# First mixer of a two-block transformer kernel: HGRN2's values third among the column groups, its states and outputs in the key's pieces

## The chip, the cores and the metric

The kernel runs on one core of a Trainium2 chip. The metric is the device time of one execution in microseconds (us), taken as the median of repeated runs. A core has TensorE (PE in the profile; its weight loads are PEld), VectorE (DVE), ScalarE (ACT), GpSimd (POOL), SyncE (SP), which here only issues transfers, and 16 DMA engines.

## The reference

Two blocks of two layers each work on a sequence of 256 tokens of width 1024, all in 32-bit floats. The change touches only the first layer of the first block, the "even mixer":

```
h = x @ w_in                                  # 1024 -> 3584 = seven groups of 512 columns
qa, ka, va, hq, hf, hi, hg = split(h)         # groups 0 .. 6
o_a = diff_attention(qa, ka, va, ...)         # 4 heads: two softmaxes, their difference times v, rms norm
o_b = hgrn2(hq, hf, hi, hg, ...)              # 4 heads, chunks of 64 tokens
mix = concat(o_a, o_b) @ w_out
```

HGRN2 is a gated linear recurrence. From `hq` and `hf` (query and forget gate) it forms decayed queries and keys per chunk of 64 tokens; with the values `hi` it forms the chunk's own output and a state that is carried from chunk to chunk; the result is rms-normed and multiplied by silu(`hg`). After the mixer come a layer norm, a feed-forward part and a gate, then the second layer, then the second block, which also has a second sequence (the "context") of 256 tokens.

## The kernel before, in words

**Tiling.** The 256 tokens are two tiles of 128 (index `t`). Every large product is computed as three fp32r matmuls (high by high, high by low, low by high), since each operand is split into a high and a low part. Weights come as units of 512 KB: `WeightStream.emit` (L208) issues the load on SP's queue, ACT casts the high part (L214), DVE subtracts to get the low part (L216). Units are consumed in program order, at most four ahead. One column group of `w_in` is a "chunk" (`chunk`, L700): four units, each 12 matmuls of 128x512 (L279 to L281), into two PSUM banks of the tag `acc`, one for each `t`. After the fourth unit the chunk's evacuation function runs for both `t`.

**Order.** The program is a list of items; an item is a unit with its matmuls, or a function without weights (`do`). `weave(a, b)` (L236) spreads the items of `b` evenly over those of `a`; with `ahead=True` the items of `b` come before the item of `a` that they are spread to. The list gives priorities only: the framework (`schedule_with_timeline_sim=True`) fixes each engine's order of instructions when the program is built, from its own estimate of times, so an item whose inputs it expects late can be passed by a later one. On the chip each engine then keeps that order.

**The even mixer** (L505) has these items beside its seven chunks:
- `hg1a`, `hg1b`, `hg1c` (L560 to L600), once for each `t`: the cumulated decays, decayed queries and keys, and masked scores. They need `hf` and `hq`. They leave three tiles of the tag `t2` for each `t` (decayed query, decayed key, masked scores).
- `hg2` (L607), once for each `t`: output of the chunk's own tokens (L613), state increments (L619), the state recurrence on DVE (L623, L626), the output from earlier states (L633), all into one `acc` bank, which ACT copies out (L636). It needs `hg1c` and the values `vv` that `evac_hi` (L602) copies out of chunk 5.
- `da`: nine items that run eight steps of differential attention, four heads with t=0 and then four with t=1, as a pipeline of two stages. `da1` (L671): scores for two softmaxes into the two `sc` banks (L676), masks and maxima on DVE (L485), exponentials on ACT (L488), the weighted difference on DVE (L678 to L680). `da2` (L683): PE transposes into the one `sm` bank and a DVE copy (L689). Item i runs `da1` of step i and `da2` of step i-1.
- `da_out(t)` (L691): the product with the values into an `acc` bank (L696), then `out_norm` (L639): squares on ACT (L420), a power on GpSimd (L385), two products on DVE (L643, L644), transposes, split into the operand of the output projection.
- `evac_hg` (L650), at the end of chunk 6: silu on ACT (L652), then `out_norm` of what `hg2` left.

**Buffers.** PSUM has eight banks: four `acc`, two `sc`, one `sm`, one `fil`. The tag `t2` has ten buffers (attention's scores, rope, norms and the tiles from `hg1` all take them), `a4` six.

**Around it.** `block1_layer` weaves fifteen further items over the mixer's list of 49: parts of the second block's modulation (`modulation`, L938: a 512 KB load each of `w_mod` into one of two `fr` buffers, matmuls L957 into `fil`) and the norm and transposes of the two context tiles (`ctx_first`'s `norm`, L1385, which also take `fr` and `fil`). The tenth and eleventh of the fifteen are the context norms, the last four are modulation. Behind the mixer's list stands the first chunk of the context's own projection (four units, 48 matmuls with input `mh`), and then the mixer's output projection `ev_w_out`.

The order that the program gives before the change: chunk 4 (`hf`), 3 (`hq`), then 0 and 1 (query, key) with `hg1` spread over them, then 2 and 5 (value, `hi`) with `da[0..5]` and `da_out(0)`, then 6 (`hg`) with `da[6..8]`, `hg2(0)`, `hg2(1)` and `da_out(1)`.

Of the kernel before, what the change touches and what calls it, by code (L numbers as in the profile page):

```python
# [119 lines left out]
def body(ctx: ExitStack, tc: tile.TileContext, A: dict, out: bass.AP):  # L120
# [112 lines left out]
    def do(fn, *args):  # L233
        return ((), lambda: fn(*args))

    def weave(a, b, ahead=False):  # L236

        out, j = [], 0
        for i, it in enumerate(a):
            if not ahead:  # L240
                out.append(it)
            while j < len(b) and (j + 1) * len(a) <= (i + 1) * len(b):
                out.append(b[j])
                j += 1
            if ahead:
                out.append(it)
        return out + b[j:]
# [20 lines left out]
    def proj(w, kdim, chunks, xs, evac, t_outer=(), tag="acc", first=0):  # L268
        new = tag if callable(tag) else lambda: PT(tag)

        items = []

        nu = kdim // 2

        def mms(o, x, wt, u):
            (xh, xl), (wh, wl) = x, wt
            for kk in range(2):
                k = 2 * ((u + first) % nu) + kk
                mm(o, xh[:, k, :], wh[:, kk, :], start=(u == 0 and kk == 0), stop=False)  # L279
                mm(o, xh[:, k, :], wl[:, kk, :], start=False, stop=False)  # L280
                mm(o, xl[:, k, :], wh[:, kk, :], start=False, stop=(u == nu - 1 and kk == 1))  # L281

        for ci, (c0, n) in enumerate(chunks):
            units = [(w, 2 * ((u + first) % nu), 2, c0, n) for u in range(nu)]
            if ci in t_outer:
                def whole(*wts, ci=ci, n=n):
                    for i, x in enumerate(xs()):
                        ps = new()[:, 0:n]
                        for u in range(nu):
                            mms(ps, x, wts[u], u)  # L290
                        evac(ci, i, ps)

                items.append((units, whole))
            else:
                held = []
                for u in range(nu):
                    def part(wt, ci=ci, n=n, u=u, held=held):
                        x = xs()
                        if u == 0:
                            held.extend(new()[:, 0:n] for _ in x)  # L300
                        for i in range(len(x)):
                            mms(held[i], x[i], wt, u)
                        if u == nu - 1:
                            for i in range(len(x)):
                                evac(ci, i, held[i])

                    items.append(([units[u]], part))
        return items
# [184 lines left out]
    def pipeline(steps, *stages):  # L493

        got = {}

        def at(i):
            for n, f in enumerate(stages):
                if 0 <= i - n < len(steps):
                    got[i - n] = f(*steps[i - n], *got.pop(i - n, ()))  # L500

        return [do(at, i) for i in range(len(steps) + len(stages) - 1)]


    def even_mixer(xs, y, ynew):  # L505
# [194 lines left out]
        def chunk(i, ev, t_outer=()):  # L700
            return proj(w, 8, [(512 * i, 512)], xs, ev, t_outer)

        da = pipeline([(h, t) for t in range(2) for h in range(4)], da1, da2)
        def consts():
# [5 lines left out]
        hf.insert(2, do(consts))  # L710
        return (
            [do(setup)] + hf + chunk(3, evac_hq)
            + weave(chunk(0, evac_q) + chunk(1, evac_k), [do(f, t) for t in range(2) for f in (hg1a, hg1b, hg1c)])
            + weave(chunk(2, evac_v) + chunk(5, evac_hi), da[:6] + [do(da_out, 0)])
            + weave(chunk(6, evac_hg), da[6:] + [do(hg2, 0), do(hg2, 1), do(da_out, 1)], ahead=True)
        ), []


# [1010 lines left out]
```

## Time and profile before

| what | value |
|---|---|
| median of 3 runs | 1923.53 us (1917.25, 1923.53, 1923.91) |
| the profiled execution: its time, its span | 1920.0 us, 1918.2 us |
| mean granted TensorE clock | 0.981 of full speed |
| PE busy | 1842.1 us, 96% of the span, 12481 matmuls |
| DVE busy | 1224.2 us, 64% |
| ACT busy | 988.7 us, 52% |
| POOL busy | 51.0 us, 3% |
| DMA | 338.84 MB, mean 177 GB/s |

The span runs from the first to the last instruction; 1.8 us of the execution lie around it. A busy share is the time in which an engine has an instruction in flight. The mixer takes roughly the first 175 us of the span.

### The profile page before, as it was taken

Reading aid. Unit: us, or ns where it says so; the run is one execution under the profiler, and the core shown is the slowest. Engines: PE = TensorE matmul, PEld = TensorE weight load, DVE = VectorE, ACT = ScalarE, POOL = GpSimd, SP = SyncE. Lnnn points to the kernel's source line nnn. Section 1 sums busy time; section 2 is a strip of 40 time slices with the busy share of each in tenths; the row PEclk is TensorE's granted clock in tenths of the full one; section 3 lists DMA queues with packets and bytes.
Section 4 is the critical chain, followed back from the end, with each engine's and each line's share of the span. In section 5 each row is a group of like instructions: output and inputs, shape, how many; then the busy total and the mean of one; then the engine's idle time right before and its main releaser. Section 6 shows DMA issues by size and latency. Waiting matters only on the chain. (4 is left out here: it accounts for less than half of the span.)

```text
span 1918.2 us, 31907 instructions
## 1 busy us (share of the span) xinstructions
PE 1842.1 (96%) x12481; PEld 1574.4 (82%) x12481; DVE 1224.2 (64%) x2333; ACT 988.7 (52%) x1630; POOL 51.0 (3%) x74
## 2 busy tenths in 40 slices
PE   7999999999999899999899999999999999989997
PEld 5766888997887688888787889899898886669997
DVE  5565656656666666668577876685646666755545
ACT  5463564554565364544568553454546556344443
POOL 1000000000000000000000000000000000000000
PEclk9999999999999899999899999999999999989999
DMA  8746654545756554465353355556665464456652
GB/s 282 253 162 212 217 184 144 176 154 192 220 167 198 191 189 151 169 219 174 118 170 103 122 163 167 168 182 192 195 212 168 153 187 146 140 177 187 184 181 98
DMA packets 100835, 338.84 MB, mean 177 GB/s; under 512 B 11572, under 2 KB 12812, under 8 KB 100684
## 3 DMA queue, kind: packets, MB, share of 16 engines
q1 hardware_dynamic: 100140, 336.43, 54.3%
q8 instruction: 98, 1.61, 0.3%
q0 software_dynamic: 544, 0.36, 0.2%
q14 instruction: 53, 0.43, 0.1%
HBM read 335.70 MB, written 1.05 MB: 176 GB/s over the span
## 5 line engine op out<-in xcount | busy, mean ns | idle before, releaser
L216 DVE TENSOR_TENSOR wl<-wr,wh 128x1024 fp32r<-128x1024 f32 (+3 forms) x562 | 638.0, 1137 | 412.6 <-ACT wh L214 406.0
L214 ACT CAST wh<-wr 128x1024 fp32r<-128x1024 f32 (+3 forms) x562 | 549.6, 981 | 655.5 <-PE acc L281 134.6
L279 PE MATMUL acc<-wh,mh 128*128 128x256 f32 (+3 forms) x400 | 132.0, 336 | 3.5 <-ACT mh L378 2.0
L280 PE MATMUL acc<-wl,mh 128*128 128x256 f32 (+3 forms) x400 | 130.8, 329 | 0.7 <-DVE wl L216 0.7
L281 PE MATMUL acc<-wh,ml 128*128 128x256 f32 (+3 forms) x400 | 131.1, 330 | 0.0
L279 PE MATMUL acc<-wh,xh 128*128 128x512 f32 (+3 forms) x304 | 117.0, 394 | 6.1 <-ACT xh L378 3.8
L280 PE MATMUL acc<-wl,xh 128*128 128x512 f32 (+3 forms) x304 | 117.9, 388 | 2.5 <-DVE wl L216 2.5
L281 PE MATMUL acc<-wh,xl 128*128 128x512 f32 (+3 forms) x304 | 117.4, 387 | 0.1
L850 PE MATMUL acc<-wh,a 128*128 128x512 f32 x256 | 102.4, 403 | 0.0
L851 PE MATMUL acc<-wl,a 128*128 128x512 f32 x256 | 101.9, 398 | 0.0
L852 PE MATMUL acc<-wh,a 128*128 128x512 f32 x256 | 101.6, 398 | 0.0
L1473 PE MATMUL sc<-xh,wh 128*128 128x256 f32 x352 | 99.7, 284 | 0.0
L1474 PE MATMUL sc<-xl,wh 128*128 128x256 f32 x352 | 99.5, 283 | 0.0
L1475 PE MATMUL sc<-xh,wl 128*128 128x256 f32 x352 | 99.5, 283 | 0.0
L1474 PE MATMUL sc<-ml,wh 128*128 128x256 f32 x352 | 99.1, 282 | 0.0
L1473 PE MATMUL sc<-mh,wh 128*128 128x256 f32 x352 | 98.9, 281 | 0.0
L1475 PE MATMUL sc<-mh,wl 128*128 128x256 f32 x352 | 98.4, 279 | 0.0
L279 PEld LDWEIGHTS acc<-wh,mh 128*128 128x128 f32 x400 | 75.2, 189 | 14.1 <-issue 3.2
L280 PEld LDWEIGHTS acc<-wl,mh 128*128 128x128 f32 x400 | 75.7, 189 | 6.6 <-DVE wl L216 1.3
L281 PEld LDWEIGHTS acc<-wh,ml 128*128 128x128 f32 x400 | 75.6, 189 | 6.7 <-issue 0.6
L279 PEld LDWEIGHTS acc<-wh,xh 128*128 128x128 f32 x304 | 58.1, 193 | 22.8 <-ACT wh L214 4.6
L825 PE MATMUL sc<-mh,wh 128*128 128x256 f32 x256 | 74.6, 293 | 1.6 <-DVE ml L358 1.6
(570 smaller groups left out, 4683.4 us busy)
## 6 DMA issues: line engine op xcount, KB each, us to landing
wr<-in_ffn_w_dram SPq DMA_DIRECT2D x128, 512.0 KB
fr<-in_w_mod_dram SPq DMA_DIRECT2D x90, 512.0 KB
wr<-in_w_gate_dram SPq DMA_DIRECT2D x66, 512.0 KB
wr<-in_w_up_dram SPq DMA_DIRECT2D x66, 512.0 KB
wr<-in_w_down_dram SPq DMA_DIRECT2D x66, 512.0 KB
wr<-in_w_in_dram SPq DMA_DIRECT2D x40, 384.0 KB
wr<-in_ev_w_in_dram SPq DMA_DIRECT2D x28, 512.0 KB
wr<-in_w_in_dram SPq DMA_DIRECT2D x28, 512.0 KB
```

The lines of the kernel that those rows point to most:

```text
L214: S.copy(hi, raw)
L216: V.tensor_tensor(lo, raw, hi, ALU.subtract)
L279: mm(o, xh[:, k, :], wh[:, kk, :], start=(u == 0 and kk == 0), stop=False)
L280: mm(o, xh[:, k, :], wl[:, kk, :], start=False, stop=False)
L281: mm(o, xl[:, k, :], wh[:, kk, :], start=False, stop=(u == nu - 1 and kk == 1))
L825: mm(o, wh[:, kk, bs], mh, start=(k == 0 and b % 2 == 0), stop=False, skip_group_check=True)
L850: mm(o, hh[:, b, ts_], wh[:, kk, :], start=(b == 0), stop=False)
L851: mm(o, hh[:, b, ts_], wl[:, kk, :], start=False, stop=False)
L852: mm(o, hl[:, b, ts_], wh[:, kk, :], start=False, stop=(b == 3))
L1473: mm(o, wh[:, kk, bs], mh, start=(k == 0 and b == 0), stop=False, skip_group_check=True)
L1474: mm(o, wh[:, kk, bs], ml, start=False, stop=False, skip_group_check=True)
L1475: mm(o, wl[:, kk, bs], mh, start=False, stop=(k == 7), skip_group_check=True)
```

## The change

Chunk 5 (`hi`) moves from fifth to third place, so that it and chunk 0 (query) carry the `hg1` items; `hg2(0)` and `hg2(1)` move from chunk 6 into chunk 1 (key); chunk 2 (value) carries the first three attention items instead of chunk 2 and 5 carrying six and `da_out(0)`; chunk 6 carries the other six, `da_out(0)` and `da_out(1)`. No instruction is added or removed by the source, and no tile or buffer count is changed.

```diff
@@ -710,9 +710,10 @@
         hf.insert(2, do(consts))
         return (
             [do(setup)] + hf + chunk(3, evac_hq)
-            + weave(chunk(0, evac_q) + chunk(1, evac_k), [do(f, t) for t in range(2) for f in (hg1a, hg1b, hg1c)])
-            + weave(chunk(2, evac_v) + chunk(5, evac_hi), da[:6] + [do(da_out, 0)])
-            + weave(chunk(6, evac_hg), da[6:] + [do(hg2, 0), do(hg2, 1), do(da_out, 1)], ahead=True)
+            + weave(chunk(5, evac_hi) + chunk(0, evac_q), [do(f, t) for t in range(2) for f in (hg1a, hg1b, hg1c)])
+            + weave(chunk(1, evac_k), [do(hg2, 0), do(hg2, 1)])
+            + weave(chunk(2, evac_v), da[:3])
+            + weave(chunk(6, evac_hg), da[3:6] + [do(da_out, 0)] + da[6:] + [do(da_out, 1)], ahead=True)
         ), []
```

Written out, with u0 to u3 for a chunk's units, the end of the mixer's list was

```
chunk 2: u0, u1, da0, u2, da1, u3, da2        chunk 5: u0, da3, u1, da4, u2, da5, u3, da_out(0)
chunk 6: da6, u0, da7, da8, u1, hg2(0), u2, hg2(1), da_out(1), u3
```

and becomes

```
chunk 1: u0, u1, hg2(0), u2, u3, hg2(1)       chunk 2: u0, u1, da0, u2, da1, u3, da2
chunk 6: da3, da4, u0, da5, da_out(0), u1, da6, da7, u2, da8, da_out(1), u3
```

The mixer's list has 49 items in both, so the fifteen items of `block1_layer` keep their places in the count: the context norms come behind items 32 and 35 (before: `da3` and chunk 5's u2; now: `da0` and chunk 2's u3), the last four modulation parts behind items 39, 42, 45 and 48.

## Rows read from the trace of the kernel before

**Rows 1.** Busy time by 10 us windows: PE, PEld, DVE, ACT, POOL, PEclk, DMA share, GB/s.
```profile
110.00:120.00 10.00, 10.00 (x47) 7.12 (x47) 4.51 (x15) 4.28 (x12) 0.57 (x1) 1.00 0.35 120
120.00:130.00 10.00, 6.69 (x31) 4.55 (x30) 7.33 (x25) 7.83 (x20) 0.56 (x1) 0.79 0.17 52
130.00:140.00 10.00, 10.00 (x60) 7.42 (x59) 8.45 (x23) 7.17 (x21) 1.02 (x1) 0.87 0.51 143
140.00:150.00 10.00, 9.86 (x76) 6.65 (x75) 7.50 (x24) 3.41 (x9) 0.00 (x0) 1.00 0.89 320
150.00:160.00 10.00, 7.50 (x64) 4.76 (x63) 2.48 (x8) 2.70 (x10) 0.81 (x1) 1.00 0.68 215
```

**Rows 2.** Waits of PE from 120 to 160 us: total, times, longest.
```profile
PE fil L177 <- ACT t L488: 2.1, 1, 2.1
PE fil L957 <- DMA fr<-in_w_mod_dram: 1.3, 2, 0.7
PE fil L177 <- DVE t L377: 1.0, 1, 1.0
PE acc L279 <- ACT t L636: 0.7, 1, 0.7
PE sm L619 <- DVE a L689: 0.5, 1, 0.5
```

**Rows 3.** Timeline of PE, 119 to 133 us: start, length, what (idle before).
```profile
119.33 0.60 PE L177 MATMUL fil<-ident,fr 128*128 128x128 f32 x4
...
122.50 0.70 PE L676 MATMUL sc<-a,a 64*128 64x256 f32 x2
123.37 0.70 PE L676 MATMUL sc<-a,a 64*128 64x256 f32 x2 [0.18 <-DVE mx L485]
126.14 1.09 PE L177 MATMUL fil<-ident,fr 128*128 128x128 f32 x4 [2.07 <-ACT t L488]
...
128.97 1.09 PE L177 MATMUL fil<-ident,fr 128*128 128x128 f32 x4 [1.02 <-DVE t L377]
129.71 0.78 PE L279 MATMUL acc<-wh,xh 128*128 128x512 f32 x1
...
132.42 0.46 PE L279 MATMUL acc<-wh,xh 128*128 128x512 f32 x1
132.72 0.40 PE L280 MATMUL acc<-wl,xh 128*128 128x512 f32 x1
132.95 0.40 PE L281 MATMUL acc<-wh,xl 128*128 128x512 f32 x1
```

**Rows 4.** Timeline of PE, end of chunk 6 to the context's projection.
```profile
141.27 0.39 PE L281 MATMUL acc<-wh,xl 128*128 128x512 f32 x1
...
156.81 0.43 PE L633 MATMUL acc<-t,t 128*64 128x128 f32 x2
157.92 0.50 PE L279 MATMUL acc<-wh,mh 128*128 128x512 f32 x1 [0.68 <-ACT t L636]
```

**Rows 5.** Timeline of ACT near 157 us.
```profile
157.28 0.59 ACT L636 COPY t<-acc 128x512 f32<-128x512 f32 x1 [9.68 <-PE acc L633]
...
158.93 1.28 ACT L652 ACT_TABLE_LOAD   x1
```

**Rows 6.** Timeline of DVE: the end of one attention step.
```profile
126.73 0.48 DVE L680 SCALAR_TENSOR_TENSOR t<-t,rs 128x256 f32<-128x256 f32 x1
...
128.75 0.41 DVE L689 COPY a<-sm 128x256 f32<-128x256 f32 x1
```

**Rows 7.** PE's modulation matmuls from 122 to 158 us, by line and form.
```profile
L957 PE MATMUL fil<-fr,cT 128*32 128x256 f32 x64 | 4.9, 390 | 1.4 <-DMA fr<-in_w_mod_dram 1.3
```

**Rows 8.** Timeline of ACT around an earlier table load.
```profile
49.55 1.04 ACT L214 CAST wh<-wr 128x1024 fp32r<-128x1024 f32 x1
50.61 1.28 ACT L567 ACT_TABLE_LOAD   x1
51.90 0.60 ACT L567 ACTIVATE t<-sm 128x512 f32<-128x512 f32 x1
```

## The prediction

> **What bounds the kernel now.** I read the windows of the first 230 us first, because the change can only act there. PE is the bound: in all eight 10 us windows from 40 to 120 us it is busy for all 10.00 us at a granted clock of 1.00 (the last of the eight stands in [rows 1]). So whatever is moved between 40 and 120 us changes nothing there: PE does the same matmuls in another order. Then come two pockets. In the window at 120 us PE is busy for 6.69 us and the clock is 0.79, in the next the clock is 0.87; at 150 us it is busy for 7.50 us.
>
> The second view is PE's waits from 120 to 160 us [rows 2]: 2.1 and 1.0 us for context transposes, 1.3 us for modulation loads, 0.7 us for ACT's copy of HGRN2's output, 0.5 us for attention's DVE copy. By the windows the idle time is 3.3 + 0.1 + 2.5 = 5.9 us [rows 1].
>
> The third is PE's timeline. **First pocket:** scores of an attention step go out at 122.50 and 123.37, then PE's queue has context transposes in front, whose input is late, and no matmul of chunk 6 ahead of them; chunk 6 starts at 129.71 [rows 3]. After that gap the clock is at the lower of its two levels (1.2 of 2.4 GHz): the first six matmuls of chunk 6 take 132.42 - 129.71 = 2.71 us, where six at the later pitch of 0.23 take 1.38, and two groups of four transposes last 1.09 us where an earlier one lasted 0.60 [rows 3]. That is 1.3 + 1.0 = 2.3 us, beside 3.3 us of idle time. **Second pocket:** chunk 6's last matmul is at 141.27; from there PE has only small matmuls until 157.92, when the context's own projection starts, right after ACT's copy of the second HGRN2 output [rows 4, 5]. In the code this is a matter of `acc` banks: chunk 6 holds two until `evac_hg` has run, which needs what `hg2` left; `hg2(0)`, `hg2(1)` and `da_out(1)` want the others; so the context's 48 matmuls, ready as far as their weights go, have no bank. Idle time here is 2.5 us.
>
> **The change, part by part.** No instruction comes or goes, so the ceiling of a gain within the mixer is what the pockets lose: 5.9 + 2.3 = 8.2 us, 0.43% of 1923.5.
>
> 1. *`evac_hi` and `hg2` go forward.* Their matmuls (L613, L619, L633) leave the second pocket and enter chunk 1, where PE is full. The dense work there moves back by as much; on PE this costs nothing and gains nothing by itself. What is gained is that at the end chunk 6's two banks are freed as soon as its silu has run, that `da_out` has a bank, and that the context's projection can go on PE while attention ends. Six of the ten `t2` buffers, which `hg1` leaves occupied until `hg2`, are free before attention starts. Of the 2.5 us of the second pocket the 0.7 us for ACT's copy and the 0.5 us for L689 [rows 2] should go; the 1.3 us for loads stay, since the last four modulation parts and the loads on SP's queue keep their place in the count. Taken: -1.2 us, between 0 and -2.5.
>
> 2. *Attention goes backward.* Five of its eight score steps and both `da_out` now stand in chunk 6; before, two score steps and one `da_out`. The serial length of a step is read from the one that starts at 122.50: its difference ends at 126.73 + 0.48 = 127.21, its copy at 128.75 + 0.41 = 129.16 [rows 3, 6], so 4.7 us to the difference and 6.7 us to the copy. Its cover is chunk 6, 141.27 - 129.71 = 11.6 us long [rows 3, 4], the modulation's 4.9 us [rows 7], four groups of context transposes of 0.6 us, 2.4 us [rows 3], and then the context's projection. If steps overlap as the two stages allow, five of them fit under 11.6 + 4.9 + 2.4 = 18.9 us, that is 3.8 us a step, and the rest under the context's 48 matmuls at 0.23 us, 11.0 us. I take 0, between 0 and the price in the rival below.
>
> 3. *Context norms keep their count.* Behind the second of them there now are four dense units (chunk 6), before five (chunk 5's u3 and chunk 6). So the first pocket can come back in another place: its cause, transposes in an in-order queue ahead of work that could run, is not removed. But chunk 6 finds `acc` banks more easily, since HGRN2's are not asked for any more, and ACT no longer has `evac_hi` between context and chunk 6. I take half of 3.3 + 2.3 = 5.6 us: -2.8, between 0 and -5.6.
>
> 4. *Loads.* All 28 units of this weight are equally big and come in equal number; SP's queue is passed by nothing but other units of the same size, and DMA share at 110 us was 0.35 [rows 1]. What hides it is the four-unit lead. Costed at 0; without that cover a late unit would show as a wait of ACT for `wr`.
>
> 5. *ACT's functions.* `evac_hg` no longer waits for `hg2`, so its silu can fall between attention's exponentials. Before, one table load of 1.28 us stands ahead of the first of these silus [rows 5]. Two changes more, there and back, would be 2.6 us on ACT, which was busy for 2.70 of 10 us at 150 us [rows 1]: hidden, unless the last step's exponential stands behind it. Around an earlier load the trace shows the copy ending at 50.59, the load at 50.61 and the next function at 51.90 [rows 8]: the load and nothing else. Against this change speaks a rule of the Trainium skill, page "ScalarE: Activation LUTs", section "Table sets: the hidden batching unit": calls are to be batched by table set. Its section "What ACT_TABLE_LOAD costs" gives some 2.66 us for a switch, with a drain that the row above does not show; an estimate by that page would be 5.3 us for the two, still less than ACT's idle time there.
>
> Sum: -1.2 + 0 - 2.8 = -4.0 us. On the profiled execution that is 1920.0 - 4.0 = 1916.0 us (span 1918.2 to 1914.2). That execution lies 3.5 us under the median of the runs, so on the median I say 1923.5 - 4.0 = **1919.5 us**. A measurement of this kernel can tell about 0.5%, 9.6 us, from no change: the borders are 1913.9 and 1933.1. The forecast is "no difference that can be told", with a lean to faster.
>
> **The rivals.**
>
> *The pockets vanish (20%).* The context's projection and the output projection fill whatever attention leaves open, and no gap is long enough for the clock to fall. For it speaks that both pockets had ready dense work without a bank or behind a blocked queue. It gives 1923.5 - 8.2 = 1915.3 us. To come below 1913.9 it needs another pocket saved later, 3.3 + 2.3 us as the first one: 1909.7.
>
> *Attention's chain is the bound at the end (slower, 18%).* Each step of chunk 6 waits until the one before is transposed and copied, because the scores' two banks, the single `sm` bank and an in-order PE queue tie them together. Then five steps take 5 x 6.7 = 33.5 us under 18.9 us of cover, 14.6 us open; the context's projection stands behind in PE's queue, the clock falls once more (2.3 us), and the present 8.2 us are replaced: 14.6 + 2.3 - 8.2 = +8.7, 1932.2 us. It decides where steps follow each other by more than 3.8 us. For it speaks that scores already wait for DVE's maxima at 123.37 [rows 3]; against it that the pipeline has two stages and that more `t2` buffers are free. With a second fall of the clock, or one more table change on the chain, it crosses 1933.1.
>
> *Exponentials and silus alternate (5%).* Four loads of 1.28 us stand on the last steps' way: +5.1 us, and the first pocket's gain of 2.8 stays: 1923.5 + 5.1 - 2.8 = 1925.8 us. The rule of the table sets named above would have it so.
>
> *Nothing changes (17%).* The order of each engine is fixed from estimated times and may already pass items by each other, and the first pocket returns with the context norms: 1923.5 us.
>
> **How the numbers follow.** The forecast has 40%: part of the pockets goes, 1917 to 1922 us. The range goes from the second pocket's gain with a further one, 1909.7, to the serial chain, 1932.2: 1909.5 to 1932. Faster by over 0.5% needs the vanishing pockets and something later: the better half of that rival and a tenth of the forecast, for shifts behind the mixer that I cannot price; 0.19. Slower by over 0.5% is some half of the chain's rival and the same kind of shift: 0.12. The rest, 0.69, is within 0.5%.
>
> **What would show it.** Steps 1 and 2: PE's timeline should have matmuls with input `mh` (L279) soon after chunk 6's last, not 16.7 us later, no wait for L636 there, and L613 to L633 inside chunk 1. Step 3: the windows from 110 to 160 us show idle time and the granted clock; idle of about 3 us and at most one fall of the clock is the forecast. Rival two shows as waits of PE for L485, L680 or L689 of several us behind chunk 6; rival three as more than one ACT_TABLE_LOAD from 100 us to the output projection. Wrong would be the whole working if PE's idle time in the mixer comes out as said and the total does not follow, that is if the windows behind 200 us, which I take as unchanged, move by more than 5 us.

## The result and the profile after

The changed kernel takes 1934.1 us (median of 4 runs, 1932.65 to 1935.76) against 1923.4 us for the kernel before: ratio 1.0069, 95% interval 1.0045 to 1.0094. It is slower by more than the 0.5% that the prediction set as the border, and 2.1 us above the upper end of the range (1932.0). The forecast was 1919.5. The lower end of the interval lies just under that border. (The two medians alone give 1.0056. The kernel before was run again beside the experiments, with medians of 1919.6 to 1921.9 us; against these 1934.1 is 1.0064 to 1.0076. Each ratio below is against the runs beside it.)

| what | before | after |
|---|---|---|
| the profiled execution: its time, its span | 1920.0, 1918.2 us | 1933.9, 1932.1 us |
| mean granted TensorE clock | 0.981 | 0.977 |
| PE busy | 1842.1 us | 1848.0 us |
| first scores of attention (L676) | 94.03 us | 115.78 us |
| last matmul of chunk 6 | 141.27 us | 131.68 us |
| maxima of the last attention step (L485) | 140.52 us | 163.15 us |
| last product with the values (L696) | 154.0 us | 171.9 us |
| first matmul of the feed-forward, layer 1 | 214.0 us | 227.6 us |
| the last matmul of that line | 422.8 us | 433.6 us |

So the loss is made in the mixer: 13.6 us at the first matmul of the feed-forward. The feed-forward gives 2.8 us back (208.8 us long before, 206.0 after), but that is not shown to be the change's doing: from 230 to 440 us PE is idle for 2.98 us in both, and the mean granted clock is 0.98 before and 1.00 after. In the profiled execution of before it fell once there (0.66 from 310 to 320 us), in that of after it did not.

The windows of PE in 10 us slices, after (columns as in [rows 1]), the answer to those rows:

```profile
110.00:120.00 10.00, 10.00 (x62) 8.12 (x61) 4.84 (x15) 6.34 (x15) 0.57 (x1) 1.00 0.32 108
120.00:130.00 10.00, 10.00 (x49) 7.91 (x48) 6.40 (x12) 6.44 (x10) 0.00 (x0) 1.00 0.52 174
130.00:140.00 10.00, 5.69 (x32) 4.14 (x30) 8.26 (x28) 7.49 (x21) 0.55 (x1) 0.75 0.64 202
140.00:150.00 10.00, 8.68 (x50) 3.56 (x50) 7.74 (x37) 3.90 (x15) 0.00 (x0) 0.67 0.64 198
150.00:160.00 10.00, 7.72 (x44) 4.18 (x43) 4.04 (x15) 2.24 (x12) 1.01 (x1) 0.72 0.61 187
160.00:170.00 10.00, 8.33 (x59) 4.93 (x58) 4.58 (x15) 1.57 (x5) 0.00 (x0) 1.00 0.43 134
170.00:180.00 10.00, 6.12 (x41) 3.58 (x40) 3.96 (x9) 4.19 (x19) 2.02 (x2) 0.83 0.66 197
```

The first pocket of before (120 to 130 us) is gone. In its place stands one of 50 us. The same view in coarser windows, the kernel before:

```profile
100.00:130.00 30.00, 26.69 (x126) 18.63 (x126) 18.55 (x67) 17.40 (x43) 1.12 (x2) 0.93 0.42 141
130.00:180.00 50.00, 47.36 (x293) 33.49 (x292) 31.86 (x74) 24.77 (x66) 4.05 (x4) 0.97 0.61 202
180.00:210.00 30.00, 29.21 (x166) 21.76 (x165) 23.39 (x36) 11.60 (x13) 2.03 (x2) 1.00 0.74 254
210.00:230.00 20.00, 19.59 (x153) 18.75 (x152) 10.91 (x13) 10.94 (x17) 0.00 (x0) 1.00 0.64 217
```

and after:

```profile
100.00:130.00 30.00, 30.00 (x174) 23.76 (x173) 16.06 (x45) 16.45 (x28) 0.57 (x1) 1.00 0.50 164
130.00:180.00 50.00, 36.55 (x218) 20.39 (x217) 28.58 (x101) 19.39 (x71) 3.59 (x4) 0.80 0.59 184
180.00:210.00 30.00, 30.00 (x152) 23.04 (x151) 20.26 (x29) 14.76 (x25) 1.01 (x1) 1.00 0.64 212
210.00:230.00 20.00, 17.02 (x88) 13.26 (x87) 17.17 (x25) 9.02 (x14) 2.02 (x2) 1.00 0.63 215
```

PE's idle time from 100 to 230 us is 3.31 + 2.64 + 0.79 + 0.41 = 7.2 us before and 13.45 + 2.98 = 16.4 us after: 9.3 us more. The lower clock, counted over the busy time, takes 26.69 x 0.07 + 47.36 x 0.03 = 3.3 us before and 36.55 x 0.20 = 7.3 us after: 4.0 us more. Together 13.3 of the 13.6 us, as an estimate from one execution of each kernel. Ahead of 100 us two more differences nearly cancel: after, PE is busy 1.5 us longer up to 40 us (30.87 against 29.37), and the clock is at 0.86 instead of 1.00 from 40 to 50 us, 1.4 us.

PE's waits after, 40 to 230 us, the answer to [rows 2]:

```profile
PE fil L958 <- DMA fr<-in_w_mod_dram: 6.8, 6, 2.3
PE fil L177 <- DVE t L377: 2.2, 1, 2.2
PE fil L177 <- ACT wh L214: 1.9, 1, 1.9
PE fil L958 <- DVE mx L485: 1.9, 1, 1.9
```

The wait for L636 is gone, as step 1 said. New are longer waits for modulation loads (6.8 us, before 1.3); 5.5 us of them lie behind 160 us. But such a wait only shows that PE had nothing else in front; what was late can be read from attention. DVE's timeline after, at the second and the seventh step's maxima:

```profile
130.00 1.23 DVE L216 TENSOR_TENSOR wl<-wr,wh 128x1024 fp32r<-128x1024 f32 x1 [1.06 <-ACT wh L214]
131.14 0.28 DVE L485 CUSTOM_DVE_ANT_0 t<-sc,cst 128x128 f32<-128x128 f32 x1
...
155.39 0.42 DVE L960 TENSOR_TENSOR gate<-fil,gate 128x256 f32<-128x256 f32 x1 [2.32 <-PE fil L958]
155.73 0.68 DVE L643 TENSOR_TENSOR t<-acc,h4stb 128x512 f32<-128x512 f32 x1
156.33 0.41 DVE L485 CUSTOM_DVE_ANT_0 t<-sc,cst 128x256 f32<-128x256 f32 x1
```

The maxima of the eight steps start at 116.31, 131.14, 138.69, 140.10, 142.96, 145.64, 156.33 and 163.15 us (before: 95.00, 100.66, 105.21, 110.48, 121.68, 129.08, 136.29, 140.52). For three of the late ones the scores were out long before: the second step's at 120.94, the third's at 132.22, the last of the seventh's at 149.42. Four gaps, of 14.8, 7.6, 10.7 and 6.8 us, make 39.9 of the 46.8 us; in between steps follow each other by 1.4 to 2.9 us. At both gaps shown the maxima stand in DVE's fixed order behind something that has nothing to do with their step. At 131.14 this is a weight unit's low part (L216), at 156.33 L643, the output norm of `da_out(0)`, and in front of that the gate of a modulation part. The last gap is of another kind: the eighth step's scores go out only at 162.41 us, behind 19 matmuls of the context's projection.

### The profile page after: what moved, and what is told of

Read it like the earlier page. It is cut to its first block, busy times and chain, and to the rows that moved or that the text cites. A ratio compares the mean times of both kernels' runs of the same rounds, so it can differ in the third digit from the quotient of the medians.

```text
span 1932.1 us, 31905 instructions
## 1 busy us (share of the span) xinstructions
PE 1848.0 (96%) x12481; PEld 1577.6 (82%) x12481; DVE 1225.9 (63%) x2333; ACT 988.3 (51%) x1630; POOL 50.9 (3%) x74
## 5 line engine op out<-in xcount | busy, mean ns | idle before, releaser
L216 DVE TENSOR_TENSOR wl<-wr,wh 128x1024 fp32r<-128x1024 f32 (+3 forms) x562 | 638.3, 1138 | 425.0 <-ACT wh L214 419.2
L1474 PE MATMUL sc<-mh,wh 128*128 128x256 f32 x352 | 98.9, 281 | 0.0
L958 PE MATMUL fil<-fr,cT 128*32 128x256 f32 x720 | 62.6, 418 | 21.5 <-DMA fr<-in_w_mod_dram 15.7
```

Source lines behind the costliest of these rows:

```text
L216: V.tensor_tensor(lo, raw, hi, ALU.subtract)
L958: mm(ps[32 * g:32 * g + 32, 0:256], cT[:, k, :], raw[:, 256 * g:256 * g + 256], start=(k == 2 * u), stop=(k == 2 * u + 1), tile_position=( ...
L1474: mm(o, wh[:, kk, bs], mh, start=(k == 0 and b == 0), stop=False, skip_group_check=True)
```

## The theories

The tile in which a step's scores are kept during the softmax has the tag `t2`. In the changed program the first context norm stands behind attention's first step, the second between the second and the third, and `da_out(0)` between the sixth and the seventh. In the trace the first writes of the tiles come in this order, whichever is ready first: the second step's scores are out at 120.94, but its maxima follow the first write of the context norm's second half (L375), as do the third step's. From the timelines of PE, ACT and DVE, after:

```profile
120.94 0.49 PE L676 MATMUL sc<-a,a 64*128 64x128 f32 x4
130.95 0.81 ACT L375 ACTIVATE t<-fil,mf 128x128 f32<-128x128 f32 x2 [0.98 <-PE fil L177]
...
138.61 0.81 ACT L375 ACTIVATE t<-fil,mf 128x128 f32<-128x128 f32 x2 [0.56 <-PE fil L177]
138.69 0.28 DVE L485 CUSTOM_DVE_ANT_0 t<-sc,cst 128x128 f32<-128x128 f32 x1
```

The maxima start at 131.14 and 138.69 us, 0.19 and 0.08 us behind these writes. By this order a buffer that comes free goes to the next tile in the program, not to the one that is ready.

- **Theory A**: the late key starts attention late, and from there the score tiles queue behind the `t2` tiles of the context norm and of `da_out(0)`. Attention ends when chunk 6's dense work is spent.
- **Theory B**: attention simply stands too late in the program; its chain of eight steps is what lasts, whatever buffers it gets.
- **Theory A2**, the bank: the context's projection is late since `evac_hg` keeps chunk 6's `acc` banks; its silu, at 174.69 us, stands on ACT behind `da_out(1)`'s squares at 172.23.
- **Theory C**: the modulation loads make the loss.
- A rival to all: the early place of HGRN2's outputs, which takes dense matmuls out of chunk 6.

## Experiments: the buffers

**Score tiles out of the queue.** On the changed kernel; `softmax_pair` makes its tile under the tag it is given. The three tags belong to later layers and lie idle here.

```diff
-            s, r = softmax_pair(ps, C("causal")[:, 256 - nk:256], nk)
+            s, r = softmax_pair(ps, C("causal")[:, 256 - nk:256], nk, ('ck1', 'ck2', 'skT')[(h + 4 * t) % 3])
```

> The changed kernel; only attention's score tiles of the first mixer leave the tag t2 and take three buffers of other tags that stand idle there. Theory A (tiles of one tag are handed out in program order, so the score tile of a step waits until the context norm's or da_out(0)'s tile before it in the program has been taken): the steps' maxima follow their scores within 2 us instead of 10 us (step 1, scores at 120.9, maxima at 131.1), five or more of the eight steps run under chunks 2 and 6, and the time falls from 1934.1 to between 1922 and 1928. Theory B (attention stands too late in the program; its chain of eight steps is what lasts): the pocket behind chunk 6 stays, 1931 or more. Theory C (loads of the modulation block PE's queue): 1931 or more, waits of PE for them stay at 6 to 7 us.

Measured: 1923.26 us, ratio to the kernel before 1.0013 (0.9998 to 1.0028). The maxima now start at 114.40, 119.12, 124.44, 129.48, 133.14, 136.07, 138.27 and 141.98 us: 27.6 us from first to last instead of 46.8. The feed-forward starts at 217.2 us. Windows of this kernel:

```profile
130.00:140.00 10.00, 8.93 (x56) 5.19 (x55) 9.10 (x37) 6.70 (x22) 0.00 (x0) 1.00 0.61 206
140.00:150.00 10.00, 6.81 (x34) 3.84 (x31) 6.53 (x25) 3.15 (x14) 1.02 (x1) 0.66 0.63 198
150.00:160.00 10.00, 8.22 (x60) 5.59 (x58) 2.24 (x5) 0.59 (x1) 0.00 (x0) 1.00 0.35 119
160.00:170.00 10.00, 8.04 (x41) 5.51 (x41) 5.24 (x11) 7.17 (x29) 2.02 (x2) 0.83 0.53 159
170.00:180.00 10.00, 10.00 (x60) 6.17 (x59) 7.39 (x11) 3.84 (x6) 1.01 (x1) 1.00 0.71 254
```

The pocket is shorter; three windows have their full clock back (130, 150 and 170 us), one has lost it (160 us, 0.83). The waits for modulation loads are still 5.7 us here, with nearly all of the time recovered, which speaks against C, and the time is far from theory B's 1931 or more. In this kernel, taking the score tiles out of the queue of `t2` tiles brings back most of the loss.

**The gate's silu tile out of the queue** (the bank), on the changed kernel.

```diff
-            gg = t2([P, 4, P])
+            gg = T([P, 4, P], F32, ("skT", "cskT")[t])
```

> The changed kernel; only the two tiles into which evac_hg's silu writes leave the tag t2. Theory A2 (the silu waits for da_out(1)'s t2 tiles and so keeps chunk 6's two acc banks, and the context's projection runs in two halves, 157.8 to 165.3 and from 177.4): both halves run in one stretch ahead of attention's last products, the idle time from 157 to 180 us (5.6 us) goes by more than half, 1934.1 falls to 1926 to 1930. The pocket from 131.9 to 157 stays as it is. Theory B: the end of attention sets the start of the output projection anyway, 1932 or more.

Measured: 1935.46 us, 1.0088 (1.0068 to 1.0109). The bank did come free earlier: the context's projection is done from 154.42 to 169.95 us (after: 157.78 to 184.2). But attention's last maxima stay at 162.38, and the hole only moves: the windows at 170 and 180 us are busy for 7.35 and 6.56 us. A2 falls as a cause of the loss.

**Both**, with only two buffers for scores.

```diff
+            s, r = softmax_pair(ps, C("causal")[:, 256 - nk:256], nk, ('ck1', 'ck2')[(h + 4 * t) % 2])
...
+            gg = T([P, 4, P], F32, ("skT", "cskT")[t])
```

> The changed kernel with both: score tiles in two buffers and the silu tiles in two buffers outside t2. Theory A with A2: both gains add, 1916 to 1923, about the kernel before or better. Theory B: 1930 or more. Theory C: not under 1927.

Measured: 1930.27 us, 1.0049 (1.0032 to 1.0067). The first seven maxima are through by 148.49, the last comes at 164.59. Theory A with A2 had 1916 to 1923. The eighth step's scores are out at 154.37, but with two buffers its tile needs that of the sixth step, whose transposes PE does at 163.84. With this one step late, 0.0036 of the 0.0056 that the first experiment brought back is missing again.

**`da_out(1)` at the very end**, on the changed kernel, which lets the silus go ahead on ACT.

```diff
-  da[3:6] + [do(da_out, 0)] + da[6:] + [do(da_out, 1)], ahead=True)
+  da[3:6] + [do(da_out, 0)] + da[6:], ahead=True) + [do(da_out, 1)]
```

> The changed kernel with da_out(1) behind chunk 6's last unit in the program instead of ahead of it; buffers as they were. Theory A2 says that the order in the program is what counts: the silus come ahead of da_out(1)'s squares on ACT, the context's projection runs on, gain like that of the separate silu tiles: 1925 to 1930. If the silu was late for another reason (its place on ACT behind the exponentials, its input), nothing changes: 1932 to 1936.

Measured: 1938.99 us, 1.0093 (1.0068 to 1.0117). The first silu comes at 156.78 us, 17.9 us earlier than after, and nothing is gained: last maxima at 162.33, and a time above both forecasts. Against A2 once more. Here ACT changed its table three times from 155 to 167 us, as the prediction's third rival had it.

**`da_out(0)` behind all attention items**, on the changed kernel, no buffer changed.

```diff
-  da[3:6] + [do(da_out, 0)] + da[6:] + [do(da_out, 1)], ahead=True)
+  da[3:] + [do(da_out, 0), do(da_out, 1)], ahead=True)
```

> The changed kernel with da_out(0) issued behind all attention items, no buffer changed. Theory A (steps 6 and 7 queue behind the output norm's t2 tiles of da_out(0)): the last step's maxima come at about 149 to 152 us rather than 163, and the time is 1924 to 1930 us. Rival (attention is late by its key alone, and what stands between its steps does not matter): the last maxima stay near 160 us and the time is 1932 to 1936 us.

Measured: 1926.57 us, 1.0033 (1.0015 to 1.0050); maxima of the seventh and eighth step at 147.23 and 151.37 us (after 156.33 and 163.15). As theory A says: where attention is late, what stands between its steps in the program has a price of its own, here some 7 us of the loss (0.0069 - 0.0033 = 0.0036 of 1921). Two windows of this kernel, for the last section:

```profile
130.00:140.00 10.00, 6.01 (x32) 3.69 (x32) 8.26 (x33) 8.16 (x25) 0.55 (x1) 0.64 0.63 208
140.00:150.00 10.00, 9.60 (x44) 3.96 (x43) 7.02 (x32) 2.18 (x8) 0.00 (x0) 0.50 0.60 176
```

## Experiments: the order

**Half of the change alone**: the column groups in the new order, HGRN2's outputs left in chunk 6. On the changed kernel:

```diff
-            + weave(chunk(1, evac_k), [do(hg2, 0), do(hg2, 1)])
+            + chunk(1, evac_k)
...
-  da[3:6] + [do(da_out, 0)] + da[6:] + [do(da_out, 1)], ahead=True)
+  da[3:6] + [do(da_out, 0)] + da[6:] + [do(hg2, 0), do(hg2, 1), do(da_out, 1)], ahead=True)
```

> Half of the change by itself: chunk 5 third, the key's chunk after the query's, attention late as in the changed kernel, but HGRN2's states and outputs left in chunk 6, behind attention's items, as before. Theory A (the late key and the handing-out order of the t2 tiles make the loss, HGRN2's move only takes cover from the end): the key is still evacuated some 16 us later than before (48 matmuls of 0.27 us and the gaps between them), so the attention's last product with the values ends at 160 us or later, the feed-forward starts by 218 to 226 us, and the time is 1925 to 1933 us. Rival (HGRN2's early place is the whole loss, the column order is free): the last product ends by 155 us, the feed-forward starts by 215 us, and the time is 1918 to 1924 us.

Measured: 1922.91 us, 1.0017 (1.0001 to 1.0033). The time is the rival's, the steps lie between: last product at 158.5 us, feed-forward from 218.5 us. PE's timeline of this kernel, attention's first scores:

```profile
106.64 0.49 PE L676 MATMUL sc<-a,a 64*128 64x128 f32 x4
```

So the column order puts attention off by 106.64 - 94.03 = 12.6 us, and HGRN2's place by another 115.78 - 106.64 = 9.1 us. What stands in these 9.1 us is seen in PE's timeline after:

```profile
89.95 0.83 PE L613 MATMUL acc<-a,t 128*128 128x128 f32 x6
...
91.05 0.39 PE L613 MATMUL acc<-a,t 128*128 128x128 f32 x2
91.37 1.16 PE L619 MATMUL sc<-a,t 64*128 64x128 f32 x8
...
95.05 1.16 PE L619 MATMUL sm<-a,t 64*128 64x128 f32 x8
...
100.39 0.83 PE L613 MATMUL acc<-a,t 128*128 128x128 f32 x6
101.15 1.09 PE L633 MATMUL acc<-t,t 128*64 128x128 f32 x8
102.17 0.49 PE L613 MATMUL acc<-a,t 128*128 128x128 f32 x2
102.59 1.16 PE L619 MATMUL sc<-a,t 64*128 64x128 f32 x8
103.67 0.43 PE L633 MATMUL acc<-t,t 128*64 128x128 f32 x2
...
110.48 1.09 PE L633 MATMUL acc<-t,t 128*64 128x128 f32 x14
...
115.78 0.49 PE L676 MATMUL sc<-a,a 64*128 64x128 f32 x4
```

The ten groups of `hg2` add up to 8.6 us, all ahead of the key's last transposes. The order alone costs 3 us, the weaving the other 10 (1.0069 against 1.0017): the part of the change that looked free is the dearer one. It delays the key, and it takes the same 8.6 us from the end, where they stood beside attention's last steps.

**Attention late in the program, the key not moved.** On the kernel before, chunk 5 ahead of chunk 2:

```diff
-            + weave(chunk(2, evac_v) + chunk(5, evac_hi), da[:6] + [do(da_out, 0)])
-            + weave(chunk(6, evac_hg), da[6:] + [do(hg2, 0), do(hg2, 1), do(da_out, 1)], ahead=True)
+            + weave(chunk(5, evac_hi) + chunk(2, evac_v), da[:3])
+            + weave(chunk(6, evac_hg), da[3:6] + [do(da_out, 0)] + da[6:] + [do(hg2, 0), do(hg2, 1), do(da_out, 1)], ahead=True)
```

> The kernel before, with one part of the change alone: attention late (three items under chunk 2, six and both da_out under chunk 6, as in the change), but query and key still carry hg1 and both hg2 stay in chunk 6. If the late attention is what costs (its score tiles then queue behind the context norms' and out_norm's tiles, and its steps run without dense cover), this is as slow as the changed kernel or slower: 1930 to 1940. If HGRN2's move into the key's chunk costs, this stays at the kernel before: 1918 to 1924.

Measured: 1919.16 us, 0.9984 (0.9972 to 0.9996). Attention's items have the late places of the changed kernel, but the first maxima come at 93.14 and the last at 139.70 us, as before; the feed-forward starts at 211.5. So "late attention is what costs" falls: that items stand late in the program costs nothing here, with the key early and HGRN2's outputs in chunk 6. This version is below both kernels, by about 3 us (1921.85 - 1919.16), less than the 0.5% of the prediction's border.

**HGRN2 among the early attention items.** On the kernel before, chunk 5 ahead of chunk 2:

```diff
+            + weave(chunk(5, evac_hi) + chunk(2, evac_v), da[:3] + [do(hg2, 0)] + da[3:5] + [do(hg2, 1), da[5], do(da_out, 0)])
+            + weave(chunk(6, evac_hg), da[6:] + [do(da_out, 1)], ahead=True)
```

> The kernel before, with the other part alone: values of HGRN2 ahead of attention's values and both hg2 taken out of chunk 6 and woven among the attention items of the two chunks before it; attention's items keep their place. If late attention is what costs, this is no slower than the kernel before: 1914 to 1923, the second pocket (141 to 158) shorter. If hg2's move costs: 1927 or more.

Measured: 1928.45 us, 1.0042 (1.0027 to 1.0057), in the range of "`hg2`'s move costs". Attention starts as early as before (first maxima 96.02) and still ends at 158.10. The same with score tiles in three buffers of their own (the expectation says a pair; the edit is that of the first experiment):

> This is the run before this one in kind (chunk 5 ahead of 2, HGRN2's states and outputs woven among the early attention items, which measured 1928.45 us, last step's maxima at 158.1 us, feed-forward from 223.3 us), with one thing more: the first mixer's attention score tiles have a pair of buffers of their own instead of queueing in the tag t2. Theory A (the loss is made by the order in which t2 tiles are handed out, so that late score tiles stand behind tiles of the context's norm): the last step's maxima end by about 135 us, the feed-forward starts by 216 us, and the time is 1914 to 1922 us. Rival (HGRN2's early outputs cost by themselves, because chunk 6 has lost 6.5 us of dense matmuls that covered attention's end): the feed-forward still starts at 221 us or later and the time is 1926 us or more.

Measured: 1936.51 us, 1.0077 (1.0058 to 1.0095), feed-forward from 228.6 us: 14 us above theory A's forecast and in the rival's range, though the last maxima are early, at 140.69. PE's timeline of this kernel shows what took their place:

```profile
155.18 1.02 PE L957 MATMUL fil<-fr,cT 128*32 128x256 f32 x8 [2.32 <-DMA fr<-in_w_mod_dram]
156.13 0.80 PE L279 MATMUL acc<-wh,mh 128*128 128x512 f32 x1
...
164.87 0.44 PE L177 MATMUL sm<-ident,skT 128*128 128x128 f32 x2
...
169.42 0.71 PE L696 MATMUL acc<-a,a 128*128 128x128 f32 x4
```

The last steps' differences are done by 146.28 + 0.48 = 146.8 us on DVE, but their transposes stand in PE's fixed order behind a modulation part that waits for its load and behind 24 matmuls of the context's projection. The second half of `hg2(1)` is late as well: its recurrence (L626) runs at 147.72, behind the context norm. So HGRN2 out of chunk 6 costs here even with early scores; whether by the cover that is missing or by the order that was fixed around it, these two runs do not separate. They do show that the last maxima are too early a mark for attention's end.

**Own score buffers on the two versions with an early key**, the same edit as in the first experiment, on the kernel before and on the one with attention late:

> The kernel before with three buffers of attention's own for the score tiles of the first mixer. Theory A: before, too, steps 4 to 7 wait for tiles of the context norms and of da_out(0); the first pocket (122 to 130 us, 5.6 us with the low clock) shrinks: ratio 0.996 to 0.999. If the order of tiles only matters where attention is late: 0.999 to 1.001.

> The kernel before with chunk 5 ahead of chunk 2 and attention late, HGRN2's outputs still in chunk 6 (measured 1919.16 us), plus score tiles in buffers of their own. Theory A: attention ends by about 130 us, and then the tail is set by HGRN2's outputs, as where the kernel before got such buffers (1922.63 us): 1918 to 1923 us, no further gain. Rival (each microsecond by which attention ends earlier comes back as time): 10 us less attention gives 1910 to 1914 us.

Measured: 1922.63 us, 1.0008 (0.9995 to 1.0020), and 1923.91 us, 1.0012 (0.9999 to 1.0026). The last maxima move from 140.52 to 127.26 and from 139.70 to 133.61 us, and no time comes back. The second is slower than its own version without the edit (0.9984), with intervals apart, as HGRN2 early was (1.0077 against 1.0042). So of four kernels that got the same buffers one is faster, one the same and two are slower: the edit helps where the late steps set the end, and it is no price of the queue by itself. With HGRN2's outputs in chunk 6 and an early key, the end is not set by the steps of attention: the last product with the values comes at 157.0 and 156.0 us, later than the 154.0 of before.

**Modulation away from the end** (theory C): on the changed kernel, the last four modulation parts go to the head of the feed-forward.

```diff
-  mix=mod(0, 0, 1) + ctx_n + mod(0, 2), first=flat(ctx_a[1:2]) + mod(0, 3),
+  mix=mod(0, 0, 1) + ctx_n, first=mod(0, 2) + flat(ctx_a[1:2]) + mod(0, 3),
```

> The changed kernel with four parts of the modulation (eight 512 KB loads and their matmuls) taken out of the mixer and put at the head of the feed-forward part. Theory C (matmuls that wait for these loads stand in PE's queue ahead of attention and the context's projection): the waits of PE for them (6.8 us up to 230 us) go, 1934.1 falls to 1924 to 1929. If attention's tiles and its chain are the cause, the pocket only has less in it: 1930 to 1936.

Measured: 1938.76 us, 1.0085 (1.0067 to 1.0102). The mixer does end earlier, the feed-forward starts at 217.8 us, but its last matmul is at 434.0 (after 433.6): what was taken out is paid there. The time lies above both forecasts. As a cause of the whole loss C falls; that the parts fill the end's queue is true. The run doesn't isolate the loads: eleven items instead of fifteen are now spread over the mixer's list, so the context norms come later too (first squares, L408, at 141.50 instead of 116.39 us), and the maxima run without a long gap from 113.20 to 140.70 us with their tiles still in `t2`.

**All kernels side by side**: the start of the first scores, of the last product with the values (L696) and of the feed-forward, in us.

| kernel | scores | last product | feed-forward | ratio |
|---|---|---|---|---|
| modulation away from the end | 112.4 | 149.6 | 217.8 | 1.0085 |
| attention late, key early | 92.6 | 151.9 | 211.5 | 0.9984 |
| before | 94.0 | 154.0 | 214.0 | 1 |
| the same as the second, own score buffers | 95.6 | 156.0 | 214.8 | 1.0012 |
| before, own score buffers | 95.4 | 157.0 | 216.7 | 1.0008 |
| column order alone | 106.6 | 158.5 | 218.5 | 1.0017 |
| changed, own score buffers | 113.9 | 160.6 | 217.2 | 1.0013 |
| changed, `da_out(0)` late | 113.8 | 166.2 | 222.0 | 1.0033 |
| HGRN2 early | 95.1 | 167.0 | 223.3 | 1.0042 |
| HGRN2 early, own score buffers | 95.8 | 169.9 | 228.6 | 1.0077 |
| changed | 115.8 | 171.9 | 227.6 | 1.0069 |
| changed, two score buffers and silu's | 117.1 | 173.8 | 225.1 | 1.0049 |
| changed, silu's buffers | 113.7 | 176.6 | 228.8 | 1.0088 |
| changed, `da_out(1)` last | 112.9 | 182.1 | 230.6 | 1.0093 |

Except for the first row, where the feed-forward got the modulation's work too, the feed-forward starts the later, the later attention's last product is, to within some 4 us. The ratio goes with the feed-forward's start, again without the first row. The start of the scores alone does not say it (113.9 and 115.8 us stand for 1.0013 and 1.0069).

## Why the prediction was wrong

**What bounds the kernel** held for PE being full from 40 to 120 us. The sentence after it, that whatever is moved there changes nothing, is the error that the failed step below rests on. PE does the same matmuls, but it matters which are done by 116 us: after, HGRN2's outputs, before, half of attention's scores.

**Step 1** (taken: -1.2 us; "on PE this costs nothing"). The wait for L636 went, and chunk 6 ended 9.6 us earlier (131.68 against 141.27). But the context's projection did not come sooner: 157.78 against 157.92 [rows 4]. Its start was held by the work in front of it. Its second half, from 177.39 us, does come earlier when the bank is free, but that brought no time (1.0088 with the silu's buffers). And the moved 8.6 us delayed the key by 9.1 us, which the step did not price. That more `t2` buffers are free, the step's last gain, did not count, since the `t2` tiles were written in program order.

**Step 2** is the step that failed: "I take 0, between 0 and the price in the rival". It asked whether five steps fit under chunk 6, and took their start for given. The start moved by 21.75 us, the last maxima by 163.15 - 140.52 = 22.6 us: attention was as long as before (46.8 against 45.5 us) and slid as a whole past the dense work that covered it. Its cover shrank too: chunk 6 was over at 131.68, by when two of eight steps had their maxima.

The step's serial length was misread as well. Lines of the kernel before:

```profile
115.23 0.70 PE L676 MATMUL sc<-a,a 64*128 64x256 f32 x2
121.68 0.41 DVE L485 CUSTOM_DVE_ANT_0 t<-sc,cst 128x256 f32<-128x256 f32 x1
...
129.08 0.41 DVE L485 CUSTOM_DVE_ANT_0 t<-sc,cst 128x256 f32<-128x256 f32 x1
...
138.98 0.48 DVE L680 SCALAR_TENSOR_TENSOR t<-t,rs 128x256 f32<-128x256 f32 x1
```

The scores at 122.50 are the sixth step's; its maxima start at 129.08 and its difference ends at 139.46. The difference that ends at 127.21 and the copy at 129.16 are the fifth step's, whose scores went out at 115.23. So from scores to difference the two took 17.0 and 12.0 us, not 4.7, and both lay some 6.5 us between scores and maxima. Before the change, too, ready scores waited; the row was there to be seen. The 6.7 us a step of the chain's rival come from the same mixture.

**Step 3** (taken: -2.8 us) was right that the pocket at 120 us goes and that it can come back elsewhere; it came back longer, 13.45 us idle from 130 to 180 us, 7.9 of them up to 160 us, where the forecast was about 3.

**Step 4.** The loads of the weight's units cost nothing new, as said: behind 41 us ACT never waits for `wr`. The modulation's loads were priced as staying at 1.3 us; they showed 6.8 us of waits, of which the experiments make a symptom: 5.7 us were left where the time was recovered.

**Step 5** was right. ACT's timeline after, at `evac_hg`, the answer to [rows 5]:

```profile
172.23 0.28 ACT L420 ACTIVATE t<-acc 128x128 f32<-128x128 f32 x1 [6.92 <-PE acc L696]
...
173.40 1.28 ACT L652 ACT_TABLE_LOAD   x1
174.69 0.60 ACT L652 ACTIVATE t<-acc 128x512 f32<-128x512 f32 x1
```

There is one load, 1.28 us long, and the silu starts 0.01 us behind it, as in [rows 8]; the silus stand behind the last exponentials. The Trainium skill, page "ScalarE: Activation LUTs", section "What ACT_TABLE_LOAD costs", gives some 2.66 us for a switch, a drain included; this trace does not show the drain. The order that alternates functions, three loads in the run with `da_out(1)` last, stood at 1.0093 against 1.0069, two intervals that overlap.

**The rivals.** "Attention's chain is the bound at the end" was the right one, with 1932.2 us against a median of 1934.1. That the number is so near is luck: its tie was another than it named, not the two score banks, the `sm` bank and PE's queue at 6.7 us a step. Where steps were free they followed each other by 1.4 to 2.9 us, below the 3.8 us from which the rival was to decide; the time went in four gaps of 6.8 to 14.8 us, three of them behind other work's tiles. Own score buffers took them away and brought back 0.0069 - 0.0013 = 0.0056 of the time, some 11 us. That "more `t2` buffers are free" stood as evidence against this rival; it was none. The chance of 0.12 for slower was too low, since the late start had no place in the sum.

**What stays open.** Each edit also changes the order that the framework fixes for every engine, as the pair with HGRN2 early shows, so the shares (3 us for the column order, 10 for the weaving, 11 back with own buffers) are those of whole kernels; they do not add up as prices of single waits. Own buffers made two other kernels slower by 0.0028 and 0.0035, half of what they brought here and more, so that the queue of `t2` tiles makes the loss is shown for the changed kernel alone, by two edits that loosen it (1.0013 and 1.0033). Why HGRN2 early stays slow with early scores is open.

## What to carry to other kernels

When work is moved into a stretch where the bounding engine is full, ask what leaves that stretch later: find the serial chain that starts from it (here the key, then eight softmax steps) and shift the whole chain by the moved work's length, then look whether cover is left at its new end. Free buffers of a shared tag help a late chain only if they are handed to it: list which tiles of the tag stand between its tiles in the program. Work that looks like filler at the end may be the cover that keeps PE and its clock up.

## What the runs showed that was not expected

The lower clock made 4.0 of the 13.3 us. It stayed at its lower level in a window that was nearly full: 9.60 of 10 us busy at 0.50 in the run with `da_out(0)` late, behind a window of 6.01 us at 0.64, with attention's and modulation's small matmuls in it.

The profiled executions differ in the clock outside the mixer, too: it fell once between 300 and 330 us before, and not after. So microseconds of a stretch are compared with its granted clock beside them.
